# Paired heads, padded queries and moved scalings in a two-block transformer kernel

## The chip, the cores and the metric

The kernel runs on one core of a Trainium2 chip (trn2). The metric is the device time of one execution in microseconds. The times shown are those of three executions and of one more that the profiler recorded.

## The reference

Two transformer blocks over 512 tokens of width 1024, all in float32. The first block is a pair of layers: 16-head "fox" attention with a forget gate, a squared-ReLU MLP, then multi-head latent attention (MLA, 8 heads) on shared keys and values, and an MLP again. The second mixes four branches (mLSTM, gated-linear attention or GLA, a conformer convolution, a short convolution) by gates, and ends in a convolutional FFN. The parts that the change touches:

```python
# fox attention: logits, a softmax over the causal keys, P @ v
f_logit = proj[..., 3 * FOX_WIDTH:] + b_f
cum = jnp.cumsum(jax.nn.log_sigmoid(f_logit), axis=1)
s = jnp.einsum('bqhd,bkhd->bhqk', q_blk, k) * scale
logits = s + c_blk - c_keys            # then causal softmax, then p @ v
# MLA: the query side
c_q = rms_norm(h @ w_q_a, q_a_norm_g)
# GLA: S_t = diag(a_t) S_{t-1} + k_t v_t^T, o_t = q_t^T S_t, 4 heads of 64
# mLSTM: C_t = f_t C_{t-1} + i_t v_t k_t^T, n_t = f_t n_{t-1} + i_t k_t,
#        h_t = C_t q_t / max(|n_t . q_t|, 1), 4 heads of 64
```

## The kernel before

Activations lie feature-major, 128 features by 512 tokens a tile. To keep float32 accuracy, each operand is split into two fp32r parts, hi and lo (`split`: ACT writes hi, DVE the remainder), and a product is three matmuls (`mm3`, L216 to L218). The weights come in 325 chunks of 128x1024: `prep` loads a chunk on SP's queue (L167), ACT writes `wh` (L181), DVE `wl` (L182); `take` hands out 128-wide slots of it. `narrow` lays hi and lo of a narrow weight side by side as 2n columns, so that two matmuls a k-tile do the work of three. PSUM has four banks called acc (projections) and four called att (everything else).

The program is written in order of the mathematics, and a scheduler then orders the instructions of each engine by their dependencies, buffers and priorities: matmuls of one projection stand between those of an attention step, as filler. So the order that runs is read from the listing of each engine, below, and not from the code.

The stages that the change touches, in us of the profiled execution:

- 0 to 52: the input norm, fox's values for heads 0 to 7 (`fox_v(0)`, token-major), the forget gate (L416, `z`, and its scan `cum`), q and k of the first pair of heads.
- 52 to 235: eight pairs of heads. `head_scores` (L328) makes four blocks of scores for each head (two matmuls each, L477 and L478, since q hi|lo and k hi, lo are packed into 128 rows), DVE adds the mask and finds the minimum (L336), ACT takes the exponential and its sum (L340), DVE the reciprocal (L342), and DVE (L346) or for block 3 ACT (L344) scales P. `head_pt` transposes P on PE (L361) and splits it; `fox_pv` multiplies by the values of the pair before (L463, L464). POOL fills half of the q tiles with a one-hot row (L440). The values of heads 8 to 15 (`fox_v(1)`) are computed after the first head's scores of pair 0.
- 630 to 676: MLA's compressed keys and queries; `normed` (L570) spreads the token factors (a matmul L300 and an ACT copy L305) and scales (L575, L230, L231); `mla_v(g)` makes the values.
- 1160 to 1190: `begin("mix")`. The token factors `rf` and `rr_` come from token sums (L283), POOL's power (L728) and L730, and are spread over 128 partitions (L731, L732). The first projection group (96 matmuls) runs on the unscaled input; its results are scaled afterwards. `modulate` (L765) builds the normed tiles `h` for the later projections.
- 1241 to 1285: GLA, in two pairs of heads. Decay-weighted keys and queries of five distances (`lev`, `kd`, `qd`) are made by DVE and ACT; per head and key block j, scores of 128, 64 and 32 wide tiles (L970, L974, L977) and two `mm3` products are written into one bank, DVE masks them, `split` makes hi and lo, `head_pv` multiplies by the values. Float32 products appear as two records each.
- 1415 to 1465: mLSTM, 4 heads of 64. q and k of the two pairs are four projections in one group; `mm3` for key block j contracts over 64 partitions, those of the head.

Of the kernel before, what the change touches and what calls it, by code (L numbers as in the profile page):

```python
# [10 lines left out]
F32 = mybir.dt.float32  # L11
# [75 lines left out]
def _body(ctx, tc, T, n_chunks, rec, dump):  # L87
# [72 lines left out]
    st = {"next": 0, "slot": 8, "cur": None, "chunk": -1, "ahead": 2, "apart": {}, "narrow": {}}  # L160
# [86 lines left out]
    def token_major(src, cols, X):  # L247
# [80 lines left out]
    def head_scores(mms, zmask, on_act=()):  # L328

        Ps = []  # L330
        for i in range(4):
# [7 lines left out]
            sume = small(1, "sume")  # L339
            act.activation(out=p, in_=ps[:, 0:n], func=AF.Exp, scale=-1.0, bias=mn, accum_out=sume)  # L340
            rs = small(1, "rs")
            dve.reciprocal(out=rs, in_=sume)  # L342
            if i in on_act:
                act.activation(out=p, in_=p, func=AF.Copy, scale=rs)  # L344
            else:
                dve.tensor_scalar(out=p, in0=p, scalar1=rs, scalar2=None, op0=ALU.mult)  # L346
            Ps.append(p)
        return Ps

    def pt_pair(j):  # L350
        n = (4 - j) * 128
        return U(f"Th{j}", F32R, n), U(f"Tl{j}", F32R, n)
# [52 lines left out]
    def fox_v(g):  # L405
        pss = token_major("fox_w_in", [(2048 + 512 * g, 512)], h)
# [188 lines left out]
    for k, w in enumerate(narrow("mla_w_kv_a", 256, 64, KT)):  # L595
# [29 lines left out]
    def mla_v(g):  # L625
        pss = token_major("mla_w_kv_b", [(hd * 256 + 128, 128) for hd in range(4 * g, 4 * g + 4)], ckv)
# [6 lines left out]
    mla_v(1)  # L633
    cq = normed(us, r, "mla_q_a_norm_g")
# [81 lines left out]
    for n in range(8):  # L716
# [4 lines left out]
               **{k: (1 if k[2] in "01" else n) for k, n in PT_TAGS.items() if k[0] == "T"})  # L721
# [9 lines left out]
    rb_h = spread(rr_, tag="misc")  # L731
    rb_f = spread(rf, tag="misc")  # L732
# [21 lines left out]
    for k in range(KT):  # L754
        for ps, cols in zip(pss, colss):
# [50 lines left out]
    psel = ph.tile([64, 256], F32R, name="psel")  # L806
    dve.tensor_copy(out=psel.rearrange("p (a b) -> p a b", a=4), in_=C("onehot", 16)[0:64, 0:4].unsqueeze(2).to_broadcast([64, 4, 64]))
# [128 lines left out]
    for p in range(2):  # L936
# [24 lines left out]
        pv = att()  # L961
        for a in range(2):
            rr = slice(64 * a, 64 * a + 64)
            PT = []
            for j in range(4):
                n = (4 - j) * 128
                b0 = j * 128
                ps = att()
# [411 lines left out]
```

## Time and profile before

| what | us |
|---|---|
| median of three runs | 2046.22 (2043.62 to 2046.45) |
| profiled execution | 2043.77 |
| its span on the core | 2042.0 |
| PE busy | 2009.4 (98%) |
| DVE busy | 1223.1 (60%) |
| ACT busy | 881.8 (43%) |
| POOL busy | 34.5 (2%) |

PE is TensorE's matmul stream and PEld its weight loads, DVE is VectorE, ACT ScalarE, POOL GpSimd, SP SyncE. Busy time adds the instructions up; matmuls overlap, so a busy PE need not be PE at its peak. A wait names the engine, the line and the tile that it waited for. PEclk is the clock granted to TensorE, as a share of full speed (2.4 GHz; the lower level is 1.2 GHz). In the timeline a row has its start, its duration, and behind it in brackets the idle time before it and who ended that.

### The profile page before, as it was taken

How to read it: one execution, taken by the hardware profiler on the slowest of the kernel's cores; microseconds unless marked ns; L12 is line 12 of the kernel's file. 1: busy time of each engine (PE TensorE's matmuls, PEld its weight loads, DVE VectorE, ACT ScalarE, POOL GpSimd, SP SyncE). 2: the span in 40 equal slices, each digit the busy share in tenths (PEclk: the TensorE clock that was granted, in tenths of full speed). 3: DMA queues.
4: the chain of work that ended last, by engine and by line, in shares of the span. 5: the costliest groups of instructions: out<-in, count | busy, mean ns of one | idle time of the engine just before them, and what ended most of it. 6: DMA issues, size and time to landing. Idle time of an engine off the chain costs nothing.

```text
span 2042.0 us, 24907 instructions
## 1 busy us (share of the span) xinstructions
PE 2009.4 (98%) x9734; PEld 1662.2 (81%) x9734; DVE 1223.1 (60%) x2050; ACT 881.8 (43%) x1436; POOL 34.5 (2%) x41
## 2 busy tenths in 40 slices
PE   8999999999999999999999999999999999999998
PEld 6777888888888778888888778888788899888887
DVE  5698764345446985633554567793835576633664
ACT  5688644224334554432343454323633455423441
POOL 0000000000000000000000000000000000000000
PEclk9999999999999999999999998999999999999999
DMA  4211354245333112632543231232122522323231
GB/s 169 83 52 52 106 178 150 93 144 176 94 102 109 42 42 93 217 101 95 176 144 93 91 128 52 63 93 83 62 87 90 164 63 68 98 95 101 93 112 64
DMA packets 61062, 210.31 MB, mean 103 GB/s; under 512 B 6912, under 2 KB 7184, under 8 KB 60944
## 3 DMA queue, kind: packets, MB, share of 16 engines
q1 hardware_dynamic: 56304, 199.99, 30.7%
q10 hardware_dynamic: 4640, 8.73, 1.3%
q8 instruction: 76, 1.25, 0.3%
q14 instruction: 42, 0.34, 0.1%
HBM read 204.50 MB, written 4.19 MB: 102 GB/s over the span
## 4 chain that ended last, share of the span: by engine, by line
PE 90%; DVE 6%; ACT 2%; issue 1%; POOL 0%; DMA 0%; DVEq 0%; POOLq 0%; SPq 0%; ACTq 0%
PE acc L216 23%; PE acc L217 23%; PE acc L218 23%; PE att L216 2%; PE att L217 2%; PE acc L1275 2%; PE acc L1277 2%; PE acc L1276 2%; PE att L218 2%; PE att L361 1%; PE acc L256 1%; PE acc L257 1%; PE acc L258 1%; DVE wl L182 1%; PE att L300 1%
## 5 line engine op out<-in xcount | busy, mean ns | idle before, releaser
L182 DVE TENSOR_TENSOR wl<-wraw,wh 128x1024 fp32r<-128x1024 f32 x313 | 382.5, 1222 | 372.7 <-ACT wh L181 363.9
L181 ACT ACTIVATE wh<-wraw 128x1024 fp32r<-128x1024 f32 x313 | 330.6, 1056 | 624.1 <-PE acc L217 485.4
L216 PE MATMUL acc<-h,wh 128*128 128x512 f32 (+1 forms) x1516 | 586.0, 387 | 1.4 <-DVE vvl L839 1.4
L217 PE MATMUL acc<-h,wh 128*128 128x512 f32 (+1 forms) x1516 | 583.9, 385 | 0.0
L218 PE MATMUL acc<-h,wl 128*128 128x512 f32 (+1 forms) x1516 | 582.6, 385 | 0.0
L216 PEld LDWEIGHTS acc<-h,wh 128*128 128x128 f32 x1516 | 285.8, 189 | 57.7 <-issue 2.2
L217 PEld LDWEIGHTS acc<-h,wh 128*128 128x128 f32 x1516 | 285.7, 189 | 55.6 <-issue 1.0
L218 PEld LDWEIGHTS acc<-h,wl 128*128 128x128 f32 x1516 | 285.7, 188 | 54.9 <-DVE wl L182 0.3
L217 PE MATMUL acc<-a,wh 128*128 128x512 f32 x512 | 199.2, 389 | 0.0
L216 PE MATMUL acc<-a,wh 128*128 128x512 f32 x512 | 199.2, 389 | 0.0
L218 PE MATMUL acc<-a,wl 128*128 128x512 f32 x512 | 199.2, 389 | 0.0
L216 PEld LDWEIGHTS acc<-a,wh 128*128 128x128 f32 x512 | 96.1, 188 | 20.0
L217 PEld LDWEIGHTS acc<-a,wh 128*128 128x128 f32 x512 | 96.1, 188 | 20.0
L218 PEld LDWEIGHTS acc<-a,wl 128*128 128x128 f32 x512 | 96.1, 188 | 19.8
L509 DVE CUSTOM_DVE_ANT_0 wada<-wada,ca 128x1024 f32<-128x1024 f32 x48 | 58.8, 1224 | 53.0 <-DMA wada<-in_adaT_dram 51.3
L527 ACT ACTIVATE tmp<-acc 128x512 f32<-128x512 f32 x64 | 37.7, 588 | 96.4 <-PE acc L218 96.4
L340 ACT ACTIVATE P<-att,mn 128x128 f32<-128x128 f32 (+1 forms) x96 | 50.6, 527 | 42.7 <-DVE mn L336 42.0
L541 DVE TENSOR_TENSOR tmp<-acc,rb 128x512 f32<-128x512 f32 x32 | 22.1, 691 | 78.3 <-PE acc L218 78.3
L1242 DVE SCALAR_TENSOR_TENSOR u<-acc,vec,u 128x511 f32<-128x511 f32 x42 | 31.4, 749 | 60.3 <-ACT u L1241 60.3
L1241 ACT ACTIVATE u<-acc,vec 128x512 f32<-128x512 f32 x42 | 28.7, 683 | 70.7 <-PE acc L218 70.7
L223 ACT ACTIVATE Th<-att 128x512 fp32r<-128x512 f32 (+1 forms) x112 | 44.2, 435 | 22.1 <-DVE att L988 16.1
L530 DVE CAST a<-tmp 128x512 fp32r<-128x512 f32 x64 | 27.3, 426 | 43.8 <-ACT tmp L528 43.7
(471 smaller groups left out, 3012.3 us busy)
## 6 DMA issues: line engine op xcount, KB each, us to landing
wraw<-in_ws_dram SPq DMA_DIRECT2D x325, 512.0 KB, 3.4
wada<-in_adaT_dram SPq DMA_DIRECT2D x48, 512.0 KB, 3.7
x<-in_xT_dram ACTq DMA_DIRECT2D x8, 256.0 KB, 3.0
x5d<-x ACTq DMA_DIRECT2D x8, 256.0 KB, 2.7
x<-x5d ACTq DMA_DIRECT2D x8, 256.0 KB, 3.3
out_dram<-xt SPq DMA_DIRECT2D x8, 256.0 KB, 2.0
ctx<-in_xT_dram SPq DMA_DIRECT2D x7, 256.0 KB, 6.1
ca<-in_c_dram ACTq DMA_DIRECT2D x2, 512.0 KB, 4.3
```

The source lines that it names most:

```text
L181: act.activation(out=h, in_=w, func=AF.Copy)
L182: dve.tensor_tensor(out=l, in0=w, in1=h.bitcast(F32), op=ALU.subtract)
L216: pe.matmul(ps, lhsT=wh, rhs=xh, start=start, stop=False)
L217: pe.matmul(ps, lhsT=wh, rhs=xl, start=False, stop=False)
L218: pe.matmul(ps, lhsT=wl, rhs=xh, start=False, stop=stop)
L223: act.activation(out=hi, in_=src, func=AF.Copy)
L340: act.activation(out=p, in_=ps[:, 0:n], func=AF.Exp, scale=-1.0, bias=mn, accum_out=sume)
L509: dve.tensor_tensor_reduce(out=w, in0=w, in1=ca["t"], scale=1.0, scalar=0.0, op0=ALU.mult, op1=ALU.add, accum_out=mod[:, i:i + 1])
L527: act.activation(out=t, in_=ps, func=AF.Relu)
L1275: pe.matmul(ps, lhsT=a[0][:, xs], rhs=wh, start=k == 0, stop=False)
L1276: pe.matmul(ps, lhsT=a[0][:, xs], rhs=wl, start=False, stop=False)
L1277: pe.matmul(ps, lhsT=a[1][:, xs], rhs=wh, start=False, stop=k == 10)
```

## The change

Lines after the first edits move by 1 to 50: L477 becomes L494, L440 L457, L361 L373, L346 L336 (the scaling, now in `scale`), L342 L356, L300 L301, L760 L781, L970/L974/L977 L1008.

- The forget gate's weights are laid out narrow: 16 matmuls for 24, then an ACT copy and a DVE add that join the hi and lo halves.
- In `head_scores`, POOL scales P in the first seven pairs, after one reciprocal of four columns a head. Pair 7 keeps DVE and ACT.
- Head 0's scores of pair 0 are issued inside `fox_v(1)`, after two of its eight k-tiles. MLA's `normed` for the queries is issued inside `mla_v(1)`, after one of two k-tiles.
- The two spreads of mix move into the projection group's loop, before k-tile 3.
- GLA: for each key block, the scores of both heads of a pair alternate, matmul by matmul, into two banks; PV for block j-1 of both heads is issued behind the scores of block j, in an acc bank. The P tiles of blocks 0 and 1 share a tag of two buffers.
- mLSTM: q of each head is written to a tile whose other 64 partitions are zero, so that all products contract over 128 partitions; the selections (`psel`, `onehot`) too. q and k of pair 1 are projected behind head 1's merges.

```diff
-    fps = project("fox_w_in", [(3072, 16)], h, att)
+    fps = att()
+    for k, w in enumerate(narrow("fox_w_in", [(3072, 16), (None, 16)], 32, KT)):
+        for i in range(2):
+            pe.matmul(fps[0:64], lhsT=w, rhs=h[k][i], start=k == 0 and i == 0, stop=k == KT - 1 and i == 1)
     z = U()[0:16]
-    dve.tensor_tensor(out=z, in0=fps[0:16], in1=rbc[0:16], op=ALU.mult)
+    act.activation(out=z, in_=fps[32:48], func=AF.Copy)
+    dve.tensor_tensor(out=z, in0=fps[0:16], in1=z, op=ALU.add)
+    dve.tensor_tensor(out=z, in0=z, in1=rbc[0:16], op=ALU.mult)
...
+    def token_major(src, cols, X, at=None, between=None):
...
         for k in range(len(X)):
+            if k == at:
+                between()
...
+        def scale(i):
+            if on_pool:
+                pool.tensor_scalar(out=Ps[i], in0=Ps[i], scalar1=rs[:, i:i + 1], scalar2=None, op0=ALU.mult)
+            elif i in on_act:
+                act.activation(out=Ps[i], in_=Ps[i], func=AF.Copy, scale=rs[:, i:i + 1])
+            else:
+                dve.tensor_scalar(out=Ps[i], in0=Ps[i], scalar1=rs[:, i:i + 1], scalar2=None, op0=ALU.mult)
...
+            if not on_pool:
+                dve.reciprocal(out=rs[:, i:i + 1], in_=sume[:, i:i + 1])
+                scale(i)
+        if on_pool:
             dve.reciprocal(out=rs, in_=sume)
-            if i in on_act:
-                act.activation(out=p, in_=p, func=AF.Copy, scale=rs)
-            else:
-                dve.tensor_scalar(out=p, in0=p, scalar1=rs, scalar2=None, op0=ALU.mult)
-            Ps.append(p)
+            for i in range(4):
+                scale(i)
...
-            Ps.append(head_scores(mms, zmask, (3,)))
+            if pr == 0 and a == 0:
+                fox_v(1, 2, lambda: Ps.append(head_scores(mms, zmask, True)))
+                continue
+            Ps.append(head_scores(mms, zmask, pr < 7, (3,)))
             if a == 0:
-                fox_v(1) if pr == 0 else fox_pv(pr - 1, PTs)
+                fox_pv(pr - 1, PTs)
...
-    mla_v(1)
-    cq = normed(us, r, "mla_q_a_norm_g")
+    cq = []
+    mla_v(1, 1, lambda: cq.extend(normed(us, r, "mla_q_a_norm_g")))
...
-    rb_h = spread(rr_, tag="misc")
-    rb_f = spread(rf, tag="misc")
...
     for k in range(KT):
+        if k == 3:
+            rb_h = spread(rr_, tag="misc")
+            rb_f = spread(rf, tag="misc")
...
+        RR = (slice(0, 64), slice(64, 128))
+        PTs = [[], []]
+        pv = acc()
+
+        def pv_block(j):
+            for a in range(2):
+                vh, vl = vg(p, a)(j)
+                mm3(pv[:, j * 128:512], vh, vl, PTs[a][j][0], PTs[a][j][1], j == 0 and a == 0, j == 3 and a == 1)
...
+            for K, Q, ks, qs, rows, cols, first, last in ops:
+                for a in range(2):
+                    pe.matmul(pss[a][rows, cols], lhsT=K[RR[a], ks], rhs=Q[RR[a], qs], start=first, stop=last,
+                              **({"tile_position": (64 * a, rows.start)} if rows.stop - rows.start == 32 else {}))
+            I32 = mybir.dt.int32
+            if j:
+                pv_block(j - 1)
+            for a, ps in enumerate(pss):
...
+                PTs[a].append(split(ps[:, 0:n], pt_pair(j)))
+        pv_block(3)
...
+    def ml_qk(p):
+
+        pss = group("w_in_2", [ct("ml_q", p), ct("ml_k", p)], h)
+        for a in range(2):
+            own = slice(64 * a, 64 * a + 64)
+            hi, lo = mqz[a]
+            act.activation(out=hi[own], in_=pss[0][own], func=AF.Copy, scale=0.125)
+            dve.scalar_tensor_tensor(out=lo[own], in0=pss[0][own], scalar=0.125, in1=hi[own].bitcast(F32), op0=ALU.mult, op1=ALU.subtract)
+        return split(pss[1], U2("mix"))
...
-                mm3(ps[:, 0:n], mk[p][0][rr, ks], mk[p][1][rr, ks], mq[p][0][rr, j * 128:], mq[p][1][rr, j * 128:], True, True)
+                mm3(ps[:, 0:n], mk[p][0][:, ks], mk[p][1][:, ks], mqz[a][0][:, j * 128:], mqz[a][1][:, j * 128:], True, True)
...
             merges(1, hd, hd + 1)
+            if hd == 1:
+                mk[1] = ml_qk(1)
```

The order that results, at three places. A row is an instruction of the engine: its line, operation, output and inputs and its size, and x4 for four alike; `ISA` is the mask pass of L336 (its second row reads the minimum out).

DVE, in a fox pair, while the scores of a head are turned into P. Before:

```order
L336 ISA att,mn<-att,zmask 128x256
L336 ISA mn 128x1
L346 TENSOR_SCALAR P_821<-P_821,rs 128x128
L342 RECIPROCAL rs<-sume 128x1
L336 ISA att,mn<-att,zmask 128x384
L336 ISA mn 128x1
L346 TENSOR_SCALAR P_832<-P_832,rs 128x256
L466 TENSOR_TENSOR tmp<-att,tmp 64x512
L342 RECIPROCAL rs<-sume 128x1
L336 ISA att,mn<-att,zmask 128x512
L336 ISA mn 128x1
L346 TENSOR_SCALAR P_843<-P_843,rs 128x384
```

In the change:

```order
L347 ISA att,mn<-att,zmask 128x128
L347 ISA mn 128x1
L347 ISA att,mn<-att,zmask 128x256
L347 ISA mn 128x1
L347 ISA att,mn<-att,zmask 128x384
L347 ISA mn 128x1
L347 ISA att,mn<-att,zmask 128x512
L347 ISA mn 128x1
L356 RECIPROCAL rs<-sume 128x4
L483 TENSOR_TENSOR tmp<-att,tmp 64x512
L347 ISA att,mn<-att,zmask 128x128
L347 ISA mn 128x1
```

The three scalings and three of the four reciprocals of a head are gone from DVE; the scaling of all four blocks waits for one reciprocal, behind the last block's exponential. On PE, 12 projection matmuls, 16 of PV and the 8 score matmuls of head 1 stand between head 0's last score and its first transpose in the change, and DVE's two passes L182 stand ahead of head 1's reciprocal and eight rows behind it.

PE, at the beginning of mix: `L283`/`L284` are the token sums, `L300`/`L301` the two spreads, the three lines of `mm3` the first projection group, `L760`/`L781` its small bias products. Before:

```order
L283 MATMUL att<-cst,tmp 128x128 x8
L216 MATMUL acc<-h,wh 128x512
L217 MATMUL acc<-h,wh 128x512
L218 MATMUL acc<-h,wl 128x512
L216 MATMUL acc<-h,wh 128x512
L217 MATMUL acc<-h,wh 128x512
L218 MATMUL acc<-h,wl 128x512
L300 MATMUL att<-cst,rr 128x128 x4
L300 MATMUL att<-cst,rtok 128x128 x4
L760 MATMUL att<-wh,shl 2x512
L760 MATMUL att<-wl,shl 2x512
L216 MATMUL acc<-h,wh 128x512
```

In the change, from the 20th row behind the token sums on:

```order
L215 MATMUL acc<-h,wh 128x512
L216 MATMUL acc<-h,wh 128x512
L217 MATMUL acc<-h,wl 128x512
L215 MATMUL acc<-h,wh 128x512
L216 MATMUL acc<-h,wh 128x512
L217 MATMUL acc<-h,wl 128x512
L781 MATMUL att<-wh,shl 2x512
L781 MATMUL att<-wl,shl 2x512
L301 MATMUL att<-cst,rr 128x128 x4
L301 MATMUL att<-cst,rtok 128x128 x4
L215 MATMUL acc<-h,wh 128x512
```

Before, six projection matmuls stand between the sums and the spreads; now 21 and six small ones do.

PE, at the beginning of GLA: `L970`, `L974`, `L977` (now all `L1008`) are the score products. Before:

```order
L218 MATMUL acc<-h,wl 128x512
L216 MATMUL acc<-h,wh 128x512
L217 MATMUL acc<-h,wh 128x512
L218 MATMUL acc<-h,wl 128x512
L970 MATMUL att<-mix 128x128 x3
L974 MATMUL att<-mix 64x64 x5
L977 MATMUL att<-mix 32x32 x4
L216 MATMUL att<-mix 128x128
L217 MATMUL att<-mix 128x128
L218 MATMUL att<-mix 128x128
L216 MATMUL att<-mix 128x256
L217 MATMUL att<-mix 128x256
```

In the change:

```order
L259 MATMUL acc<-wh,h 128x256
L1008 MATMUL att<-mix 128x128 x3
L1008 MATMUL att<-mix 64x64 x4
L1008 MATMUL att<-mix 128x128
L1008 MATMUL att<-mix 64x64
L1008 MATMUL att<-mix 32x32 x8
L1008 MATMUL att<-mix 128x128 x6
L1008 MATMUL att<-mix 128x256 x6
L1008 MATMUL att<-mix 64x64 x3
L1008 MATMUL att<-mix 32x32 x8
L1008 MATMUL att<-mix 128x256 x6
L215 MATMUL acc<-Th_10168,vvh 128x512
```

Nine projection matmuls stood before the first score product and now none (the row ahead is the last of the values); the products of two heads alternate, which the listing shows as doubled counts, and PV of block 0 follows the scores of blocks 0 and 1, in an acc bank. Of 25 fillers inside the stage, three are left.

## Rows read from the trace of the kernel before

**Rows 1.** The page, busy time of each engine, its share of the span, instructions.
```profile
PE 2009.4 (98%) x9734; PEld 1662.2 (81%) x9734; DVE 1223.1 (60%) x2050; ACT 881.8 (43%) x1436; POOL 34.5 (2%) x41
```

**Rows 2.** Waits of PE, whole span: total, times, longest us.
```profile
PE acc L216 <- ACT c L230: 2.4, 1, 2.4
PE att L477 <- ACT x L451: 2.1, 1, 2.1
...
PE acc L216 <- DVE vvl L839: 1.4, 1, 1.4
PE att L300 <- DVE rr L730: 1.2, 1, 1.2
```

**Rows 3.** Windows: us, then busy of each engine, PEclk, DMA share, GB/s.
```profile
50.00:60.00 10.00, 7.36 (x29) 5.32 (x28) 6.32 (x13) 7.12 (x13) 0.00 (x0) 0.83 0.31 106
100.00:200.00 100.00, 98.78 (x502) 76.77 (x501) 89.00 (x243) 83.64 (x195) 7.37 (x10) 1.00 0.17 53
1167.00:1191.00 24.00, 24.00 (x112) 17.96 (x111) 22.64 (x35) 14.03 (x20) 0.00 (x0) 1.00 0.43 148
1241.60:1285.00 43.40, 41.96 (x347) 33.40 (x346) 27.84 (x73) 15.95 (x32) 0.00 (x0) 0.81 0.12 37
1410.00:1430.00 20.00, 20.00 (x88) 15.57 (x86) 8.07 (x14) 11.83 (x20) 0.00 (x0) 0.91 0.17 54
```

**Rows 4.** Timeline of PE, gate stage: start us, us, instruction; first and next projection.
```profile
34.37 0.40 PE L216 MATMUL att<-h,wh 128*16 128x512 f32 x1
...
39.92 0.39 PE L216 MATMUL att<-h,wh 128*128 128x512 f32 x1
```

**Rows 5.** Lines of DVE, ACT, 100 to 200 us: busy, mean ns | idle before.
```profile
L346 DVE TENSOR_SCALAR P<-P,rs 128x256 f32<-128x256 f32 (+2 forms) x30 | 10.6, 354 | 0.0
...
L342 DVE RECIPROCAL rs<-sume 128x1 f32<-128x1 f32 x39 | 6.3, 161 | 5.1 <-ACT P L340 4.7
...
L344 ACT ACTIVATE P<-P,rs 128x512 f32<-128x512 f32 x10 | 7.1, 711 | 0.3 <-DVE rs L342 0.3
```

**Rows 6.** Waits, 100 to 200 us, one of PE's weight loads.
```profile
PEld att L477 <- ACT P L340: 3.8, 10, 0.5
```

**Rows 7.** Timeline of POOL and DVE, fox pairs.
```profile
157.76 0.61 POOL L440 CAST x<-onehot 64x512 fp32r<-64x512 f32 x1 [12.69 <-PE att L478]
...
198.07 0.61 POOL L440 CAST x<-onehot 64x512 fp32r<-64x512 f32 x1 [12.71 <-PE att L478]
...
204.47 1.21 DVE L182 TENSOR_TENSOR wl<-wraw,wh 128x1024 fp32r<-128x1024 f32 x1
...
204.68 1.48 POOL L440 CAST x<-onehot 64x512 fp32r<-64x512 f32 x1 [6.00 <-PE att L478]
```

**Rows 8.** Timeline of ACT and DVE, MLA norm.
```profile
666.68 0.60 ACT L305 ACTIVATE tmp<-att 128x512 f32<-128x512 f32 x1 [0.59 <-PE att L300]
...
667.61 0.68 DVE L575 TENSOR_TENSOR qk<-qk,tmp 128x512 f32<-128x512 f32 x1
...
668.32 0.72 ACT L230 ACTIVATE c<-qk,vec 128x512 fp32r<-128x512 f32 x1 [0.55 <-DVE qk L575]
```

**Rows 9.** Timeline of DVE, first modulation of mix.
```profile
1167.31 0.69 DVE L765 TENSOR_TENSOR tmp<-x,misc 128x512 f32<-128x512 f32 x1 [1.77 <-ACT misc L305]
```

**Rows 10.** Timeline of PE, GLA: last value matmul, two score products, after the end.
```profile
1241.50 0.28 PE L258 MATMUL acc<-wh,h 128*128 128x256 f32 x1
...
1247.58 0.28 PE L217 MATMUL att<-mix 64*128 64x256 f32 x1
...
1247.70 0.27 PE L218 MATMUL att<-mix 64*128 64x256 f32 x1
...
1285.00 0.63 PE L217 MATMUL acc<-h,wh 128*128 128x512 f32 x1
```

**Rows 11.** Timeline of PE, mLSTM: wide matmuls around three of 64 rows.
```profile
1436.67 0.40 PE L216 MATMUL acc<-h,wh 128*128 128x512 f32 x1
...
1437.81 0.40 PE L218 MATMUL acc<-h,wl 128*128 128x512 f32 x1
```

More of the change, by code (lines that the diff above doesn't have):

```diff
@@ L157, in _body @@
     act.activation(out=mod[:, 0:16], in_=mhalf, func=AF.Copy)
-    st = {"next": 0, "slot": 8, "cur": None, "chunk": -1, "ahead": 2, "apart": {}, "narrow": {}}
+    st = {"next": 0, "slot": 8, "cur": None, "chunk": -1, "ahead": 2, "apart": {}, "narrow": {4: (KT, 32)}}
     ready = []
@@ L351, in pt_pair @@
         n = (4 - j) * 128
-        return U(f"Th{j}", F32R, n), U(f"Tl{j}", F32R, n)
+        t = j if f"Th{j}" in phase["tags"] else "01"
+        return U(f"Th{t}", F32R, n), U(f"Tl{t}", F32R, n)
     def head_pt(Ps):
@@ L623, in _body, with mla_v @@
     vt = {}
-    def mla_v(g):
-        pss = token_major("mla_w_kv_b", [(hd * 256 + 128, 128) for hd in range(4 * g, 4 * g + 4)], ckv)
+    def mla_v(g, at=None, between=None):
+        pss = token_major("mla_w_kv_b", [(hd * 256 + 128, 128) for hd in range(4 * g, 4 * g + 4)], ckv, at, between)
         for s in range(4):
@@ L720, in _body @@
     ph = begin("mix", mix=14, gate=3, y=8, mo=2, misc=7,
-               **{k: (1 if k[2] in "01" else n) for k, n in PT_TAGS.items() if k[0] == "T"})
+               **{k: n for k, n in PT_TAGS.items() if k[0] == "T" and k[2] in "23"}, Th01=2, Tl01=2)
     rf = rsqrt_tok(sums[0], D)
@@ L1009, in _body @@
     merges(3, 2, 8)
-    pss = group("w_in_2", [ct("ml_q", 0), ct("ml_k", 0), ct("ml_q", 1), ct("ml_k", 1)], h)
-    mq, mk = [None, None], [None, None]
-    for p in range(2):
-        mq[p] = split_s(pss[2 * p], 0.125, U2("mix"))
-        mk[p] = split(pss[2 * p + 1], U2("mix"))
+    mqz = [[U("mix", F32R) for _ in range(2)] for _ in range(2)]
+    for a in range(2):
+        other = slice(64 - 64 * a, 128 - 64 * a)
+        for t in mqz[a]:
+            pool.tensor_copy(out=t[other], in_=zero[other, 0:1].to_broadcast([64, S]))
+    def ml_qk(p):
+        pss = group("w_in_2", [ct("ml_q", p), ct("ml_k", p)], h)
+        for a in range(2):
+            own = slice(64 * a, 64 * a + 64)
[3 more added lines that the diff above has]
+        return split(pss[1], U2("mix"))
+    mk = [ml_qk(0), None]
     vm = values([(O["ml_v"], 256)], True)
@@ L1047, in _body @@
         ps = att()
-        pe.matmul(ps, lhsT=psel[0:64, p * 128:(p + 1) * 128], rhs=mr[0:64], start=True, stop=True)
+        pe.matmul(ps, lhsT=psel[:, p * 128:(p + 1) * 128], rhs=mr, start=True, stop=True)
         em = U("mix")
@@ L1055, in _body @@
             mps = att()
-            pe.matmul(mps, lhsT=onehot[0:64, hd:hd + 1].to_broadcast([64, 128]), rhs=Mr[0:64], start=True, stop=True)
+            pe.matmul(mps, lhsT=onehot[:, hd:hd + 1].to_broadcast([128, 128]), rhs=Mr, start=True, stop=True)
             Mm = U("mix")
```

71 lines of the change are left out of this document (27 added, 44 removed).

## The prediction

> **What bounds the kernel now.** I read the busy line first: PE is busy 98% of the span, DVE 60%, POOL 2% [rows 1]. So nothing is gained by lighter work on DVE, ACT or POOL as such; time goes only where PE waits, where PE is granted half of its clock, where it issues matmuls more slowly than their columns need, or where it issues matmuls that can be left out. The waits of PE show the first kind: of the ones the change touches, 2.1 us before the first fox scores, 2.4 before the MLA projections, 1.2 before the mix spreads and 1.4 beside GLA [rows 2]. The table of windows shows the second: the mean granted clock is 0.83 in 50 to 60 us, 0.81 in the GLA stretch and 0.91 in 1410 to 1430 us, and 1.00 in 100 to 200 us [rows 3]. A clock of 0.81 is a mix of the two levels, 2.4 and 1.2 GHz. The third kind is seen only in the timeline, from start to start: a 512-column fp32r matmul normally follows the one before it after 0.23 us, for the busy figures hide slow issue.
>
> **The change part by part** (minus is time saved). The sum stands against the profiled execution, 2043.8 us, which lies 2.4 us below the median of the three runs (2046.2).
>
> *Forget gate.* Its 24 matmuls take 34.37 to 39.92 us, 5.55 us or 0.231 each [rows 4]. With hi and lo weights side by side there are 16: 8 x 0.231 = **-1.8**. One ACT copy and one DVE add are new; they run beside the q and k projections that follow on PE.
>
> *Start of the fox attention.* PE is busy 7.36 us of 50 to 60 us, so 2.6 us are waited, and a clock of 0.83 costs 10 x 0.17 = 1.7 us [rows 3]. The change puts head 0's scores behind 24 value matmuls (24 x 0.23 = 5.5 us), more than the 2.1 us that the score matmuls wait for ACT [rows 2]. If the pause goes, so does the dip behind it: 2.6 + 1.7 = **-4.3**. It is -2 if the clock falls nevertheless.
>
> *Fox pairs 1 to 7.* Two pairs take 198.07 - 157.76 = 40.31 us by one POOL row that recurs once a pair [rows 7], 20.2 us a pair. By columns a pair needs less: 48 projection matmuls, and 16 score and 16 PV matmuls of mean 320 columns (10 + 10 full ones), 68 x 0.231 = 15.7, and 20 transposes of 128 columns, at 0.12 each as a 256-column product in GLA [rows 10], 2.4, together 18.1. So 2.1 us a pair are lost to waits for buffers and tiles. In 100 to 200 us DVE is busy 89.0 and ACT 83.6 of 100 us [rows 3], and weight loads wait for P on ACT (one line: 3.8 us) [rows 6]; that is a stage where DVE and ACT, each in order, pace PE. The change takes 10.6 us of scaling by L346 and most of 6.3 us of reciprocals off DVE and 7.1 us of scaling by L344 off ACT, per five pairs [rows 5]: 3.2 and 1.4 us a pair. DVE would then be busy about 73%. POOL takes 1280 columns a head on instead. Its nearest row is a copy of 512 columns: 0.61 us alone, and 1.48 where it runs beside DVE's L182, which starts at 204.47 and reads two SBUF tiles [rows 7]. That gives 1280/512 x 0.61 = 1.5 us, or 3.7. The chain for head 0 is then a mask pass and an exponential over 512 columns, taken at the 0.71 of L344, a reciprocal of 0.16 [rows 5] and POOL's 1.5 to 3.7: 3.1 to 5.3 us. In the new order 12 projections, 16 PV and 8 score matmuls stand between head 0's last score and its first transpose, 27 x 0.231 = 6.2 us, and some 8 us for head 1; so the chain is covered at both ends. I take half of the 2.1 us a pair as won, since the other waits (k tiles, PSUM banks) stay: 7 x 1.0 = **-7**. Ends: 0, if the transposes in one block cost what the scaling saved, and -15 (all of it).
>
> *MLA norm.* The wait is 2.4 us [rows 2]. Now 12 matmuls (2.7 us) of the second value projection cover the chain of L305's copy 0.60, L575 0.68, L230 0.72 [rows 8] and a DVE pass for lo like L575's, together 2.7 us. The cover is barely as long as the chain: **-1.8**, between 0 and -2.4.
>
> *Mix spreads.* The wait of 1.2 us for rr goes [rows 2]. But the spreads move behind 21 projection matmuls and 6 small ones, 27 x 0.23 = 6.2 us after the token sums, where before it was 6 matmuls (1.4 us) and the wait of 1.2: the spread comes 3.6 us later. Behind it is DVE: L765 at 1167.31 us opens the modulation [rows 9], and DVE is busy 22.64 of the 24 us from 1167 to 1191 [rows 3], while the next projections need what it writes. A chain that fills its engine ends later when it starts later. PE meanwhile is ahead by 1.2 us and runs out of work sooner. Ends: -1.2 (the wait simply goes) and +3.6 (the whole delay shows). I take **+2**, as the DVE row is so nearly full: this step loses.
>
> *GLA.* From the end of the values to the last PV the stage takes 1285.00 - 1241.6 = 43.4 us [rows 10]. In it 1.4 us are a wait [rows 2], and at a clock of 0.81 [rows 3] 0.19 x 43.4 = 8.2 us are lost. Of the remaining 33.8 us, 25 filler projections take 5.7 and 48 PV matmuls of mean 320 columns 48 x 0.144 = 6.9; so 21.2 us are the 272 records of 64-row score products. A 256-column one starts 0.12 us after its neighbour [rows 10], that is already near its columns; the 128-column ones cost about the same. The change interleaves the two heads, whose rows lie in partitions 0 to 63 and 64 to 127, and moves 22 of the 25 fillers (5.0 us) out of the stage to where they cost the same. If the two halves run side by side, the scores take 10.6 us, PE gets faster than DVE (27.84 us busy in the stage), the stage ends at about 1241.6 + 27.8 + 1 = 1270.4, and the gain is 14.6 - 5.0 = 9.6. If they don't, the gain is the wait of 1.4 us and half of the switches between tile widths, less what DVE's splits make PE wait for with the fillers gone: 0 to -3, or a loss of 2. I take **-5.5**, the middle between 9.6 and 1.4, for no row of this trace shows two halves in flight.
>
> The Trainium skill, TensorEngine Tiling (Array Packing), section Key Properties, says that different tiles can execute weight loads and matmuls in parallel; by that, -9.6 would stand in the sum (a rival below). No row here shows it.
>
> *mLSTM.* Between 1436.67 and 1437.81 us stand one wide matmul, three of 64 rows and 128 columns, and one wide one [rows 11]: 1.14 us, where 2 x 0.23 and 3 x 0.12 would be 0.82. With queries padded to 128 rows this 0.32 us goes, in 16 such places, of which some 14 stand between wide ones: 4.5. The columns streamed stay the same. The dip of 0.09 x 20 = 1.8 us in 1410 to 1430 us [rows 3] may go. Against it: the second pair's q and k come later, beside head 1, and per pair one half-tile pass more on ACT and on DVE (each at most the 0.71 us of L344 [rows 5]), some 0.8 us on the path in all. **-5.5**, between -3 and -7.
>
> Sum: -1.8 - 4.3 - 7 - 1.8 + 2 - 5.5 - 5.5 = -23.9. Against the profiled execution that is 2019.9, against the median 2022.3; I say **2021**.
>
> **Rivals.**
> 1. *GLA gives nothing* (halves don't run side by side, DVE paces). For: the clock of 0.81 stays where PE is held up by DVE, and the fillers that covered it go. Against: the wait and the switches. Sum -18.4: 2025.4 from the profiled execution, 2027.8 from the median; 2026.5.
> 2. *GLA runs at DVE's pace and the fox pairs win 1.5 us each*: -9.6 and -10.5 in place of -5.5 and -7, sum -31.5: 2012 to 2015; 2013.5. For: DVE at 89% in the fox stage. Against: the PSUM and k waits that stay. This is the rival that goes by the rule on tiles.
> 3. *Slower: POOL becomes the pace of the fox pairs.* It decides once four scalings take more than the cover less the chain, 6.2 - 1.6 = 4.6 us for head 0 and some 6.4 for head 1. The row at 0.61 us has 64 partitions; if 128 double it and DVE's two-tile reads slow it by 1.48/0.61 = 2.4, a head costs 1.5 x 2 x 2.4 = 7.3 us: PE waits 2.7 + 0.9 us in each of 7 pairs, 25 us. The -7 goes too: -23.9 + 7 + 25 = +8, 2052. For: the row at 1.48. Against: in the new order DVE's passes over two SBUF tiles mostly stand before a head's reciprocal, not behind it, so POOL scales alone. The Trainium skill, GPSIMD Engine Reference, section Elementwise, keeps elementwise work on DVE and gives GpSimd about 2.6 cycles an element, so 2.8 us a head as an estimate at its 1.2 GHz; by that POOL stays inside the cover. Its section Specifications says that the SBUF interfaces are shared with VectorE when an instruction of that reads two SBUF inputs; the 1.48 us row agrees.
> 4. *The start of fox stays as it is* (the scheduler keeps the pause or puts another in the values): -23.9 + 4.3 = -19.6, close to rival 1: 2025.
>
> **How the numbers follow.** Forecast 0.55, rival 1 0.18, rival 2 0.16, rival 3 0.04, rival 4 0.05; 0.02 for anything else. The bounds: low is rival 2 less another 5 us for ends of the other terms, 2008; high is rival 1 with the weak ends of the fox pairs or mLSTM (some 6.5 us), 2033. Faster or slower counts from 0.2%, 4.1 us, about what runs of this kernel tell apart (they span 2.8 us). All cases but rival 3 are over 4 us faster: 0.93 faster; 0.04 for no difference, were several terms at their weak ends at once; 0.03 slower.
>
> **What would show it.** Gate: 16 matmuls. Fox start: no wait of about 2 us before the first scores, clock near 1.00 in 50 to 60 us. Pairs: two L457 rows two pairs apart by about 38 us, four POOL scalings a head, DVE near 73% busy in 100 to 200 us, no wait of transposes for POOL. Mix: no wait for rr, but the first modulation near 1171 us after a shift by what was saved ahead, and PE waiting for DVE around the end of the group. GLA: score starts of the two heads closer than 0.12 us, DVE the releaser. mLSTM: no step beyond 0.23 and 0.12 us between products. The forecast is wrong if POOL appears in PE's waits, if the pairs keep 20 us, or if GLA's stage is longer than 38 us.

## The result and the profile after

The changed kernel takes 2023.76 us (median of four runs, 2022.69 to 2025.42) against 2045.88 us before (2043.62 to 2046.45): the ratio is 0.9895, 95% interval 0.9877 to 0.9912, so it is faster by 1.05%, about 22 us. The forecast was 2021. The kernel before also ran beside the experiments, at medians of 2048.3 to 2050.73 us, so the profile of before that the steps below are taken against (2043.77 us) is one of its quicker executions. The profiled span went from 2042.0 to 2020.8 us, 21.2 less. By stage, from the start of the same instruction in both traces (a negative number is time saved up to there; the last column is the step between two marks):

| mark | before | after | difference | step | forecast |
|---|---|---|---|---|---|
| first PV of pair 0 (L463, now L480) | 98.12 | 92.89 | -5.2 | gate and fox start -5.2 | -6.1 |
| first MLA product (L597, now L617) | 630.14 | 623.03 | -7.1 | fox pairs -1.9 | -7 |
| `rr` of mix (L730, now L750) | 1165.20 | 1153.96 | -11.2 | MLA -4.1 | -1.8 |
| last GLA factor of pair 0 (L960, now L981) | 1245.41 | 1235.83 | -9.6 | mix +1.7 | +2 |
| first head norm behind GLA (L849, now L870) | 1295.27 | 1278.82 | -16.5 | GLA -6.9 | -5.5 |
| mean behind mLSTM (L1108, now L1149) | 1522.74 | 1501.56 | -21.2 | mLSTM -4.7 | -5.5 |

The sum came out 2.7 us short of the forecast's -23.9; two terms are far off, the fox pairs (too high) and MLA (too low), and cancel in part, so that the total came so near is partly luck. The busy line of the page after, against [rows 1]:

```profile
PE 1986.6 (98%) x9726; PEld 1654.3 (82%) x9726; DVE 1210.8 (60%) x1969; ACT 872.7 (43%) x1425; POOL 94.8 (5%) x101
```

POOL works 94.8 us where it worked 34.5; PE is as full as before. The waits of PE after (total, times, longest):

```profile
PE att L1008 <- DVE mix L971: 4.9, 3, 3.2
...
PE acc L215 <- DVE h L223: 2.4, 1, 2.4
...
PE att L807 <- ACT tmp L804: 1.6, 1, 1.6
...
PE att L494 <- DVE x L469: 1.0, 1, 1.0
...
PE att L373 <- POOL P L336: 0.6, 1, 0.6
```

Of the four waits of [rows 2], those for `vvl` and `rr` are gone, and the 2.1 us for `x` became 1.0; that of MLA is there with its 2.4 us, but on another tile (`h`, a value bank, in place of `c`). GLA waits 4.9 us for DVE, and a new wait of 1.6 us is in mix. The windows that answer to [rows 3] (columns as there):

```profile
50.00:60.00 10.00, 9.03 (x43) 7.31 (x42) 7.35 (x16) 8.44 (x17) 0.61 (x1) 1.00 0.20 57
100.00:200.00 100.00, 97.79 (x511) 78.99 (x510) 82.41 (x189) 80.44 (x191) 49.18 (x51) 1.00 0.17 54
1156.00:1180.00 24.00, 22.40 (x108) 17.20 (x107) 21.34 (x38) 13.83 (x20) 0.00 (x0) 0.98 0.37 132
1179.00:1183.00 4.00, 4.00 (x12) 3.14 (x11) 3.92 (x9) 2.02 (x4) 0.00 (x0) 0.57 0.25 63
1231.92:1275.00 43.08, 38.00 (x376) 29.63 (x375) 29.83 (x80) 17.08 (x34) 2.75 (x4) 0.88 0.12 38
1391.00:1411.00 20.00, 20.00 (x98) 16.65 (x97) 15.63 (x24) 16.30 (x32) 0.00 (x0) 1.00 0.16 53
```

At the start of fox PE is busy 9.03 of 10 us and the clock is 1.00, for 7.36 and 0.83. In 100 to 200 us DVE fell from 89.0 to 82.4, and not to the 73 of the forecast. The window of GLA is as long as the one before and reaches beyond the stage, which now ends 11.7 us sooner after its values (1231.92 to 1263.67 for 1241.6 to 1285.00; 22 fillers, 5.0 us, stand behind it now and not in it). The stage alone has a mean clock of 0.84, for 0.81 before:

```profile
1231.92:1263.67 31.75, 26.67 (x326) 20.22 (x324) 27.43 (x73) 14.44 (x31) 2.75 (x4) 0.84 0.11 35
```

Around mLSTM the clock is 1.00 for 0.91. But there is a stretch at half clock in mix that was not there, at 1179 to 1182.4 us.

### The profile page after: what moved, and what is told of

It reads as the page before. It is cut to its first block, busy times and chain, and to the rows that moved or that the text cites. A ratio compares the mean times of both kernels' runs of the same rounds, so it can differ in the third digit from the quotient of the medians.

```text
span 2020.8 us, 24983 instructions
## 1 busy us (share of the span) xinstructions
PE 1986.6 (98%) x9726; PEld 1654.3 (82%) x9726; DVE 1210.8 (60%) x1969; ACT 872.7 (43%) x1425; POOL 94.8 (5%) x101
## 3 DMA queue, kind: packets, MB, share of 16 engines
q8 instruction: 76, 1.25, 0.2%
## 4 chain that ended last, share of the span: by engine, by line
PE 90%; DVE 7%; ACT 2%; issue 1%; POOL 0%; DMA 0%; ACTq 0%; DVEq 0%; POOLq 0%; SPq 0%
PE acc L215 23%; PE acc L216 23%; PE acc L217 23%; PE acc L1316 2%; PE acc L1318 2%; PE acc L1317 2%; PE att L215 2%; PE att L216 2%; PE att L217 2%; PE att L373 1%; PE acc L257 1%; PE acc L258 1%; PE acc L259 1%; DVE wl L182 1%; PE att L301 1%
## 5 line engine op out<-in xcount | busy, mean ns | idle before, releaser
L182 DVE TENSOR_TENSOR wl<-wraw,wh 128x1024 fp32r<-128x1024 f32 x312 | 381.5, 1223 | 377.9 <-ACT wh L181 369.3
L294 POOL TENSOR_TENSOR rtok<-mst,mhalf 128x4 f32<-128x4 f32 (+1 forms) x12 | 11.3, 945 | 1114.6 <-DVE mst L292 1114.6
L336 POOL TENSOR_SCALAR P<-P,rs 128x128 f32<-128x128 f32 (+3 forms) x56 | 60.2, 1092 | 30.2 <-DVE rs L356 30.2
```

Source lines behind the costliest of these rows:

```text
L182: dve.tensor_tensor(out=l, in0=w, in1=h.bitcast(F32), op=ALU.subtract)
L336: pool.tensor_scalar(out=Ps[i], in0=Ps[i], scalar1=rs[:, i:i + 1], scalar2=None, op0=ALU.mult)
```

## The experiments

Each ratio compares with the kernel before, run beside that experiment on the same chip. Against the change, which was not run again there, the comparison goes by stage, between the marks of the table.

**GLA.** The question was which part of the pairing gave the 6.9 us, and what held the stage up. First the heads in turn against one after the other (x3):

```diff
-            for K, Q, ks, qs, rows, cols, first, last in ops:
-                for a in range(2):
+            for a in range(2):
+                for K, Q, ks, qs, rows, cols, first, last in ops:
```

> The changed kernel with the score products of the two GLA heads of a pair issued one head after the other for each key block, not in turn. Theory: in turn, two products in different halves of the rows start 3 to 7 ns apart and share a slot of about 0.11 us; one head after the other, each takes its own slot, PE's time for the products doubles (about 21 us in place of 10.6), part of it under DVE's own time in this stage. The time rises by 3 to 6 us, to 2027 to 2030. Rival: DVE sets the pace of the stage anyway, and the products' order changes under 1 us.

Measured: 2046.89 us, ratio 0.9989 (0.998 to 0.9998). That is 23 us more than the change by the medians and some 19 by the ratios, most of the whole gain, and over three times the upper end of what was expected. The windows of x3 show where it went (columns as in [rows 3]):

```profile
1240.00:1250.00 10.00, 10.00 (x64) 6.91 (x63) 5.28 (x14) 2.31 (x4) 0.00 (x0) 0.50 0.00 0
1250.00:1260.00 10.00, 10.00 (x62) 7.48 (x61) 5.33 (x13) 2.52 (x7) 1.92 (x3) 0.50 0.16 52
1260.00:1270.00 10.00, 7.65 (x75) 6.25 (x74) 6.14 (x13) 3.68 (x7) 0.87 (x2) 0.50 0.16 54
1270.00:1280.00 10.00, 10.00 (x57) 7.28 (x57) 3.77 (x10) 1.75 (x4) 0.00 (x0) 0.50 0.01 2
```

The clock is granted at half, 1.2 GHz, through the whole stage, 54.6 us on end, which costs 27 us. The mean clock of the span is 0.983 to 0.986 in all eleven runs of x3 and 0.993 to 0.995 in the four of the change, so this goes with the order and not with one execution. The changed kernel, with the same products two by two, in the same stretches:

```profile
1240.00:1250.00 10.00, 9.76 (x95) 7.09 (x93) 8.63 (x24) 4.70 (x13) 2.36 (x4) 0.81 0.00 0
1250.00:1260.00 10.00, 8.35 (x116) 6.30 (x116) 8.26 (x18) 3.11 (x6) 0.39 (x1) 0.83 0.33 107
1260.00:1270.00 10.00, 10.00 (x76) 8.26 (x75) 3.97 (x19) 2.80 (x6) 0.00 (x0) 1.00 0.01 2
1270.00:1280.00 10.00, 10.00 (x46) 8.28 (x45) 3.01 (x4) 4.02 (x6) 0.00 (x0) 1.00 0.31 105
```

From L981 to L870 (L960 to L849 before) GLA takes 67.0 us in x3 and 43.0 in the change, 24.0 more. The change has 10.2 us at half clock there, 44.4 less than x3, and half of that is 22.2 us. By this sum some 2 us are left for the products that no longer run side by side. The expectation had the direction, but nearly all of the price is the clock, which it left out.

Then PV in an att bank in place of an acc bank (x4):

```diff
         PTs = [[], []]
-        pv = acc()
+        pv = att()
```

> The changed kernel with GLA's PV accumulated in an att bank, as before the change, and not in an acc bank. Theory: with PV in an acc bank, projections of later stages find no acc bank and can't fill PE's waits of 3.2 and 1.5 us in GLA; in the order with PV in att nine projections stand before the first score again. Then the 4.9 us of waiting for DVE in GLA become work, but the score products have one att bank less and wait for DVE's splits. If the first weighs more, the time falls by 2 to 4 us, to 2020 to 2022, with less half clock in GLA. Rival: the att bank is what the alternation needs; the two halves fall apart again in the order and the time rises by 1 to 4 us.

Measured: 2019.5 us, ratio 0.9853 (0.9838 to 0.9868); the profiled span is 2015.9, 4.9 us below the change (3.4 of it in GLA and 1.9 behind mLSTM, where the profile of the change has a stretch at half clock at 1660 us and this one has none; 0.4 were lost ahead of GLA). In its order nine projections stand before the first score product again, and its trace shows no wait of PE for GLA's factors beyond 0.2 us and no half clock in the stage:

```profile
1240.00:1250.00 10.00, 9.47 (x90) 6.91 (x89) 8.57 (x21) 4.83 (x12) 1.25 (x2) 1.00 0.17 52
1250.00:1260.00 10.00, 9.15 (x97) 6.33 (x95) 8.23 (x16) 4.03 (x7) 1.81 (x3) 1.00 0.32 107
1260.00:1270.00 10.00, 10.00 (x99) 8.00 (x98) 5.32 (x22) 2.40 (x7) 0.00 (x0) 1.00 0.01 2
1270.00:1280.00 10.00, 10.00 (x54) 8.60 (x53) 4.13 (x8) 5.42 (x7) 0.00 (x0) 1.00 0.15 54
```

```profile
PE acc L215 <- DVE vvl L860: 1.4, 1, 1.4
...
PE att L215 <- DVE Tl L223: 0.9, 2, 0.5
...
PE att L1008 <- DVE mix L971: 0.2, 1, 0.2
```

From L960 to L849, 49.9 us before, GLA takes 43.0 us in the change and 39.6 in x4. So the pairing is good for 10.2 us, and the bank of PV gave a third of it back. The clock is most of it: the 17.0 us of half clock in the stage before, 8.5 us of time, are gone in x4. At full clock all through, the old stage would be some 2 us longer than that of x4, by an estimate from these figures. The paired GLA alone in the kernel before, with PV in acc (x8, the edit is GLA's part of the change):

> The kernel before with the paired GLA alone (PV in an acc bank). Theory: the gain of the stage by itself, 6 to 7 us (span 2035 to 2036), with some half clock left in the stage, as in the changed kernel. Rival: the gain depends on where the stage starts; with more than 13 us of half clock it is under 4 us.

Measured: 2035.5 us, ratio 0.9926 (0.9913 to 0.994), span 2034.6: 7.4 us less. Of it 5.9 lie before L849, with 17 us of half clock in the stage, and 1.5 in mLSTM, whose dip of [rows 3] was not there in this run. The rival's condition, over 13 us of half clock, came true, but not its gain of under 4 us. By the ratio the gain is 15 us, twice that of the profiles: the kernel before took 2050.73 us beside x8, and the half clock in its GLA varies (last section).

**The fox stage.** x6 takes the start alone, x9 one tile of sums alone, x2 takes the scaling off POOL, and x7 leaves it out.

```diff
+            if pr == 0 and a == 0:
+                fox_v(1, 2, lambda: Ps.append(head_scores(mms, zmask, (3,))))
+                continue
             Ps.append(head_scores(mms, zmask, (3,)))
             if a == 0:
-                fox_v(1) if pr == 0 else fox_pv(pr - 1, PTs)
+                fox_pv(pr - 1, PTs)
```

> The kernel before with one edit: head 0's scores of pair 0 inside the second value projection; scaling on DVE and ACT with a tile of sums per block, as before. Theory: the pause and the half clock at 56 to 60 us go, 3.4 to 4.3 us less, span 2038 to 2039; and the later pairs keep their 20.2 us, since the order of their transposes stays in pieces. Rival: the start shifts all pairs and they too go to 19.5 to 19.7 us; then it is 6 us or more.

Measured: 2042.01 us, ratio 0.9964 (0.9952 to 0.9977). PV of pair 0 starts at 94.36 for 98.12 us, 3.8 less, and the lead stays 3.7 to 3.8 to the end of the stage: the pairs keep 20.2 us. The ratio would make it 7 us, and the profiled span is longer than before, 2047.1: both go with the half clock in GLA, 34.1 us in this profile, and not with fox (last section).

```diff
+        sume, rs = small(4, "sume"), small(4, "rs")
         for i in range(4):
...
-            sume = small(1, "sume")
...
-            rs = small(1, "rs")
-            dve.reciprocal(out=rs, in_=sume)
+            dve.reciprocal(out=rs[:, i:i + 1], in_=sume[:, i:i + 1])
```

> The kernel before with one edit: the sums and reciprocals of a head's four blocks lie in one 128x4 tile; DVE and ACT scale P block by block as before. In the order this alone puts nine of a head's ten transposes in one run, where before they stood in four to six pieces. Theory: that order, and not the work taken off DVE, is what shortened the pairs: the period goes from 20.2 to 19.7 us, as in x2, and the fox stage is 3 to 4 us shorter. Rival: the shift at the start of fox makes it; the period stays at 20.2 us.

Measured: 2044.32 us, ratio 0.9983 (0.9968 to 0.9998), span 2037.8. The pairs take 19.7 us (POOL's recurring row, a pair apart), and nine or all of a head's ten transposes stand in one run:

```profile
135.92 0.61 POOL L439 CAST x<-onehot 64x512 fp32r<-64x512 f32 x1 [13.22 <-PE att L477]
...
155.65 0.61 POOL L439 CAST x<-onehot 64x512 fp32r<-64x512 f32 x1 [13.20 <-PE att L477]
```

Up to L597 the trace is 2.4 us shorter, 0.9 of it ahead of the first PV of pair 0, with all the work still on DVE and ACT; 3 to 4 were expected. x2, the changed kernel with the scaling back on them:

```diff
-                fox_v(1, 2, lambda: Ps.append(head_scores(mms, zmask, True)))
+                fox_v(1, 2, lambda: Ps.append(head_scores(mms, zmask, False, (3,))))
...
-            Ps.append(head_scores(mms, zmask, pr < 7, (3,)))
+            Ps.append(head_scores(mms, zmask, False, (3,)))
```

> The changed kernel with P scaled by DVE and ACT in all pairs, one reciprocal a block, as before the change. Theory: the scaling on POOL is worth what the pair period shows, 20.2 to 19.5 us, some 0.7 us a pair and 3 to 5 us in all: the time rises to 2027 to 2029, and a pair takes 20.0 to 20.3 us. Rival 1: the pairs gain from the order of transposes and not from the scaling: the time stays at 2024. Rival 2: POOL's 4.3 us a head hold the pairs up and DVE would do as well: the time falls.

Measured: 2024.05 us, ratio 0.9873 (0.986 to 0.9887). At L617 it stands 7.1 us before the kernel before, as the change does. Its window of 100 to 200 us:

```profile
100.00:200.00 100.00, 98.70 (x509) 78.33 (x508) 89.10 (x249) 86.00 (x200) 6.11 (x10) 1.00 0.17 54
```

DVE is at 89.1 of 100 us, as before the change, and the pairs take 19.7 us (POOL's rows recur at 131.34, 151.06 and 170.77). Rival 1 is what came. So 0.5 of the 0.7 us a pair are owed to the one tile of sums and the order that it makes, and POOL adds 0.2. One pair in the change takes 20.2 us and gives most of that back. POOL's rows of the changed kernel show it:

```profile
131.00 0.61 POOL L457 CAST x<-onehot 64x512 fp32r<-64x512 f32 x1 [5.63 <-PE att L495]
134.09 4.26 POOL L336 TENSOR_SCALAR P<-P,rs 128x128 f32<-128x128 f32 x4 [2.48 <-DVE rs L356]
...
150.48 0.61 POOL L457 CAST x<-onehot 64x512 fp32r<-64x512 f32 x1 [5.62 <-PE att L495]
153.92 4.67 POOL L336 TENSOR_SCALAR P<-P,rs 128x128 f32<-128x128 f32 x4 [2.83 <-DVE rs L356]
...
170.64 0.61 POOL L457 CAST x<-onehot 64x512 fp32r<-64x512 f32 x1 [5.96 <-PE att L495]
```

A pair is 19.48 us from 131.00 to 150.48 and 20.16 from 150.48 to 170.64. In the second, the four scalings of the first head take 4.67 us, and the wait of 0.6 us for `P` on POOL is there. x7 leaves the scaling out:

```diff
         if on_pool:
             dve.reciprocal(out=rs, in_=sume)
-            for i in range(4):
-                scale(i)
```

> The changed kernel with the scaling of P in the first seven pairs left out altogether (the reciprocal stays); the first attention's output is thus not normalised. Theory: DVE and POOL were no bound any more, and PE's own order sets the pair: the period stays at 19.4 to 19.5 us, and only the pair in which POOL ran beside DVE's L182 loses its 0.65 us; the time falls by 0.5 to 1.5 us against the changed kernel. Rival: POOL's 4.3 us a head are what the pair waits for: the period falls to 18.1 to 18.8 us, and the time by 5 to 9 us.

Measured: 2023.03 us, ratio 0.9869 (0.9855 to 0.9882). The pairs take 19.43 to 19.56 us, all of them. At L617 it stands 8.2 us before the kernel before, 1.0 more than the change, 0.65 of it the one slow pair. With no scaling anywhere the other pairs are what they are with POOL's 4.3 us a head: the scaling sets them on neither engine. PE's waits in 100 to 200 us of x7 are these, and the trace of before lists none there:

```profile
PE att L478 <- ACT P L350: 1.6, 5, 0.3
```

**Mix.** x1 puts the spreads back ahead of the group:

```diff
-        if k == 3:
-            rb_h = spread(rr_, tag="misc")
-            rb_f = spread(rf, tag="misc")
```

> The changed kernel with the two spreads of mix put back ahead of the projection group; all else stays. Theory: moving them cost more than the wait of 1.2 us that it removed, since the modulation on DVE starts later and PE then runs dry (1.6 us waiting for ACT's bias row, then a stretch at half clock that costs 1.7 us). Undone, the wait of about 1.2 us for rr is back, the other two are gone, and the time falls by 1 to 2.5 us against the changed kernel, so 2021 to 2023 us. Rival: the loss in mix comes from elsewhere (the order of the projections): then the time rises by the 1.2 us, to about 2025.

Measured: 2024.83 us, ratio 0.9878 (0.9865 to 0.9892), span 2022.5, 1.7 us more than the change and not less. The time is what the rival gave, about 2025, but the stage says otherwise. In mix the theory holds: from L750 to GLA's L981 the stage takes the 80.2 us of the kernel before, 1.7 us less than in the change; its waits there are one, of the 1.2 us that had gone:

```profile
PE att L301 <- DVE rr L750: 1.2, 1, 1.2
```

But GLA, which starts 0.5 us sooner, was at half clock for 17.1 us where the change had 10.2: its step is -4.8 us for -6.9. The question of the spreads is thus settled by their stage, and not by the total. The 1.7 us have two parts: in x7, which keeps the spreads in the loop and the wait of 1.6 us, mix has no half clock and takes 0.5 us more than before, not 1.7. So the moved spreads cost about 0.5, and the half clock the rest.

**MLA.** The norm inside the second value projection, alone (x10; the edit is the change's):

> The kernel before with MLA's query norm issued inside the second value projection, and nothing else. Theory: the wait of 2.4 us for c is replaced by one of the same size for the acc banks of the values, whose split on ACT and DVE queues behind the norm; what the changed kernel gains in MLA (3.7 us) comes from the order of the first heads behind it. So the MLA stage is 3 to 4 us shorter with a PE wait of about 2.4 us still there. Rival: the gain in MLA came from the shifts of the stages ahead; alone, the edit gives under 1.5 us.

Measured: 2046.75 us, ratio 0.9991 (0.9981 to 1.0002), no difference that can be told. From L597 to L730 the trace is 1.8 us shorter, and there is a stretch of 3.4 us at half clock at 671 us, so it would be 3.5 without. The wait is as expected:

```profile
PE acc L216 <- DVE h L224: 2.4, 1, 2.4
```

x9 above shortens the same stretch by 3.1 us with no edit in it but the tile of sums: MLA's eight heads use `head_scores` too. So either edit alone is worth some 3 us here (x10 by the estimate without its half clock), and together they give 4.1; the second the forecast did not count at all. How the two overlap was not tried.

**mLSTM.** x11 is the change's padded queries alone:

> The kernel before with the zero-padded queries of mLSTM alone (128-row selections, q and k of pair 1 later). Theory: 4.5 to 5.5 us less in the stage (no extra time at the change between 64-row and 128-row products, no half clock near 1418 us). Rival: part of it is owed to GLA's shift; alone 2 to 3 us.

Measured: 2044.9 us, ratio 0.9978 (0.9964 to 0.9992). From L849 to L1108 it is 4.7 us shorter, the same as in the change. The ratio agrees, 4.5 us; only the profiled span, 2044.6, does not show it, with 30.7 us of half clock in GLA. A part is the dip near 1418 us: it is absent in x6, x8 and x9 too, where mLSTM is as before, and the stage is 1.5 us shorter there. So the padding itself is good for 3.2 us. In the change the products follow each other without the steps of [rows 11]:

```profile
1390.36 0.40 PE L217 MATMUL att<-mix 128*128 128x512 f32 x1
1390.60 0.33 PE L215 MATMUL att<-mix 128*128 128x384 f32 x1
1390.76 0.34 PE L216 MATMUL att<-mix 128*128 128x384 f32 x1
...
1391.12 0.40 PE L215 MATMUL acc<-h,wh 128*128 128x512 f32 x1
1391.36 0.40 PE L216 MATMUL acc<-h,wh 128*128 128x512 f32 x1
```

**A version that beats both.** x5 joins x4 and x1; x12 also issues MLA's norm ahead of the value projection (`mla_v(1, 0, ...)` for `mla_v(1, 1, ...)`).

> The changed kernel with PV of GLA in an att bank (as in x4) and the spreads of mix ahead of the group (as in x1). Theory: the two effects lie in different stages and add: against x4, 1.7 us less in mix (the wait of 1.6 us for ACT's bias row and the half clock at about 1180 us go, the wait of 1.2 for rr is back), and GLA stays at full clock; span 2014 to 2015 us, about 1.5% under the kernel before. Rival: the shift of the start puts GLA back into half clock, as in x1 (13.7 us of it); then the span is 2016 to 2020.

> The kernel of x5 with MLA's query norm issued ahead of the second value projection's first k-tile, so that 24 matmuls (5.5 us) stand behind its spread and the splits of the values come after it. Theory: the wait of 2.4 us for the acc banks shrinks to under 1 us, span 2012 to 2013 us. Rival: ACT and DVE stay the bound between the norm, the chunk and the splits, and the wait moves to the next products: the span stays at 2014 to 2016.

Measured: x5 2018.3 us, ratio 0.9843 (0.9829 to 0.9856), span 2014.5; x12 2015.36 us, ratio 0.9844 (0.9823 to 0.9864), span 2013.3. Both are some 1.6% under the kernel before, and the two can't be told apart by time. The span of x5 is as expected. That of x12 is just above what was, and its wait in MLA, under 1 us by the expectation, is 1.0:

```profile
PE acc L215 <- DVE h L223: 1.0, 1, 1.0
```

## Why the prediction was right, and where it was not

- *Forget gate and fox start* held. The 16 matmuls take 33.97 to 37.65 us, 0.23 each; the start gave 3.8 alone (x6), between the -4.3 taken and the end of -2.
- *Fox pairs* failed at the step "that is a stage where DVE and ACT, each in order, pace PE". DVE was busy 89% and that was read as a bound. x2 keeps it at 89% and is as short as the change in this stage; x7 takes the work away altogether and gains 1.0 us. The waits of PE spoke against it before the change: in 100 to 200 us the trace of before lists none of its matmuls, only weight loads [rows 6]. The floor of 18.1 us a pair was also too low: a pair takes 19.5 us with the scaling gone, and PE's listed waits are 0.3 of that; what slows the rest was not separated. POOL's price was outside its ends, 4.27 us a head for 1.5 to 3.7, and the cover of 6.2 us just held it: 1.6 + 4.3 = 5.9, but for one pair. The one head whose scalings took 4.67 us, over the 4.6 at which rival 3 decides, made PE wait 0.6 us. That is one of the forecast's own signs of being wrong, POOL in PE's waits; by its sum some 0.3 us more a head would have made every pair wait. Two pairs take 39.0 to 39.6 us, where it gave 38.
- *MLA* came out right in sign for a wrong reason: the wait did not shrink. It changed its tile, since the splits that free the value banks now queue behind the norm on ACT and DVE. In x12, where the norm comes first, the wait is 1.0 us, which bears this out. What was won lies in the heads behind it, in part through the 128x4 tile in `head_scores` (x9), which I had put down for fox alone, and there for its work and not for its order.
- *Mix* held in its number, +1.7 for +2, but only in part by the mechanism that was told. The modulation starts later, PE runs out of filler, and it waits 1.6 us for ACT's bias row in place of 1.2 for `rr`: that costs 0.5 (x7). The half clock behind the wait makes up the rest and was not foreseen, so the size is luck.
- *GLA* held in size, -6.9 for -5.5, between the 1.4 and the 9.6 of which the forecast took the middle. The halves do run side by side, the point on which rival 2 rested: six 256-column products take 0.56 us in the change, where three took that before, from the first row here to the end of the one at 1247.70 us [rows 10].

```profile
1247.41 0.33 PE L216 MATMUL att<-mix 64*128 64x256 f32 x1
```

```profile
1253.24 0.56 PE L1008 MATMUL att<-mix 64*128 64x256 f32 x6
```

The Trainium skill's TensorEngine Tiling (Array Packing), section Key Properties, which lets different tiles run in parallel, is borne out by this row. The stage takes 31.75 us with DVE busy for 27.43, where the forecast had 28.8 by DVE's pace: PE stood idle 4.9 us for DVE with no filler at hand, and 10.2 us went at half clock. With as much half clock as before (17.0 us, in x1, x2, x7 and x8) the step is only 4.8 to 5.7 us, so 1 to 2 of the 6.9 are the clock. The forecast's 9.6 has all of the 8.2 us of lost clock in it as won, and 5.1 were still lost. The forecast saw that the fillers leave the stage but put it down as neutral ("to where they cost the same"). It was not: x4 brings them back, with full clock in the stage, and gains 3.4 us there.
- *mLSTM* held: -4.7 for -5.5, the same alone and with the rest. By x6, x8 and x9 the dip is 1.5 of it (1.8 taken), and the padding 3.2, where 4.5 less 0.8 were taken.
- *The range* held because errors of both signs met, which is luck in part. That GLA would give nothing (rival 1) and that POOL would make it slower (rival 3) did not happen.

## What to carry to other kernels

An engine that is busy 89% beside a PE at 99% is a bound only if PE's waits say so. Take the work out in a trial before it is moved to another engine. A bank, or a tile made wider, is an edit of the order too, wherever a scheduler decides it; PV's bank cost 3.4 us here and a 4-wide tile of sums gave 5.5 over two stages (2.4 and 3.1 in x9). Judge an edit of a few microseconds by its own stage, between two marks in the traces, when another stage's clock varies from run to run; and look for half clock inside that stage too before its step is put down to the edit.

## What the runs showed of the hardware that was not expected

The clock of TensorE decides more than any wait here, and it varies with the same code. GLA as it was before was at half clock for 17.0 us in the profile of before, and for 34.1, 27.2, 23.8 and 30.7 in x6, x9, x10 and x11, which don't touch it: 8.5 to 17 us of time. With paired heads and PV in acc it was 10.2 us in the change, 17.1 in x1, 17.0 in x2, x7 and x8; with PV in att none in x4, x5 and x12. The mean clock in 1230 to 1300 us, of x6 and then of x5:

```profile
1230.00:1300.00 70.00, 68.55 (x471) 56.34 (x470) 39.75 (x99) 25.67 (x46) 0.00 (x0) 0.76 0.10 33
```

```profile
1230.00:1300.00 70.00, 67.14 (x519) 52.91 (x518) 55.59 (x116) 27.65 (x49) 6.82 (x5) 1.00 0.19 61
```

In x6 PE counts as busy 68.55 of 70 us, more than in x5, and is granted 0.76; the busy share does not tell it. What came before a fall in these traces was a wait of PE or a run of narrow products (in the change it fell at 1237.0 us, after 3.2 us of waiting and in the 64- and 32-wide products); what came before the rises was not singled out.

POOL's price for a scaling of 128 partitions by a scalar of each is not that of its copy (64 partitions by 512 columns, 0.61 us): 128 to 512 columns take 0.60, 0.92, 1.25 and 1.60 us.

```profile
L336 POOL TENSOR_SCALAR P<-P,rs 128x512 f32<-128x512 f32 x14 | 22.3, 1595 | 0.0
L336 POOL TENSOR_SCALAR P<-P,rs 128x384 f32<-128x384 f32 x14 | 17.4, 1245 | 0.0
L336 POOL TENSOR_SCALAR P<-P,rs 128x256 f32<-128x256 f32 x14 | 12.9, 924 | 0.0
...
L336 POOL TENSOR_SCALAR P<-P,rs 128x128 f32<-128x128 f32 x14 | 8.5, 604 | 30.2 <-DVE rs L356 30.2
```

That is 0.33 us for each 128 columns and 0.27 at the start. DVE took 0.42 us for 384 columns before, a third of POOL's 1.25:

```profile
L346 DVE TENSOR_SCALAR P<-P,rs 128x384 f32<-128x384 f32 x10 | 4.2, 416 | 0.0
```

The Trainium skill's GPSIMD Engine Reference, section Elementwise, gives about 2.6 cycles an element for an operation on two input tensors, at a clock of 1.2 GHz; that makes 0.28 us for 128 columns by an estimate. The scaling reads one tensor and a column of scalars, and the runs show a little more for it, and a start for each instruction on top. So the forecast's 2.8 us a head, which used the figure for this operation, was too low for the 4.27 measured.
